# High and low weight tiles ahead of the token tiles, and two of the second feed-forward's five pairs in a pool of its own

## The chip, the cores and the metric

The kernel runs on one core of one Trainium2 chip. The metric is the device time of one execution in microseconds (us); lower is better. Engines are named as in the profile: PE is TensorE, DVE is VectorE, ACT is ScalarE, POOL is GpSimd, SP is SyncE, which issues the loads of the weights.

## The reference, cut to what matters

One block on 256 tokens of width 2048, in fp32: a feed-forward (width 5632), a mixer (S5 recurrence and pooling), cross attention to 256 memory tokens, a second feed-forward, and a last norm. The change touches the place of the weight tiles in all of it, and the work of the second feed-forward and its surroundings:

```python
def swiglu(x, w_gate, w_up, w_down):
    return (jax.nn.silu(x @ w_gate) * (x @ w_up)) @ w_down
...
    return o @ w_o          # end of the memory cross attention
```

The block ends as h = h + 0.5 * swiglu(rmsnorm(h), w2_gate, w2_up, w2_down), and then the last rmsnorm.

## The kernel before, in words

Every fp32 product is made of three products of rounded parts: a high part (fp32r) and the low rest. Weights come from HBM as 1 MB tiles `raw` (pool `wraw`, three buffers, 24 KB of each partition), by loads that SP issues (line 147). Each is split in two halves of 256 columns by `parts` (lines 136 to 143): ACT makes the high half `whi` by a copy (line 140), DVE the low half `wlo` by a subtraction (line 141). One `whi` with its `wlo` is called a pair here; each takes 8 KB of a partition. A pair feeds twelve matmuls in `tok_block` (lines 149 to 156: 2 blocks of columns x 2 halves of the tokens x 3 products, lines 154, 155, 156), with a token or activation tile `x` as the stationary operand and the weights as the moving one, 512 wide. In the middle of the block `load_w` and `block` (lines 103 to 120) use the same buffers the other way round, with the weights stationary.

Tile pools lie one behind the other in each partition, in the order in which they are opened: `const`, `wraw`, `xp` (16 token tiles of 2 KB), `actp` (12 activation tiles of 2 KB), `ev` (small buffers), and then `whl` with three pairs. Before the second feed-forward `whl` is closed (line 1008) and a pool `whl2` of five pairs is opened in its place (line 1009); a tile of a new pool waits until all users of the old one's room are done.

The order of instructions on each engine is set by a scheduler from dependencies and pools; it is not written out by hand. Semaphore waits follow from that order.

The end of the cross attention (lines 999 to 1003) is four groups of w_o; each ends with `add_to_h` (lines 256 to 262: DVE adds two accumulators to `h`) and `squares` (lines 231 to 236: ACT, names evq and ssq). `layer_in` (lines 244 to 254) transposes `h` on PE (line 251) into the next stage's token tiles.

The second feed-forward has eleven chunks f of 512 columns. Chunks 0 and 1 go through `plain` (line 1023). The other nine go through `seven` (line 1088), in which sums of quarters let seven products do the work of eight: `product` (lines 1055 to 1062) takes six matmuls from a pair, with quarters of token tiles or the sums `SH` and `SL` as the stationary operand; `eight` (line 1106) is the plain way for the rest. `SH`, `SL` and the temporaries lie in a pool `sw` behind the others (line 1067). Down passes for finished chunks are taken in between (accumulators `dacc`). The last down pass, of chunk 10 alone, runs after `sw` is closed (line 1177): four groups n of one raw tile, eight pairs in all, each group followed by `add_to_h` (line 262), `squares` and, one group later, `columns` (lines 1167 to 1175: eight transposes, four copies `o`).

Of the kernel before, what the change touches and what calls it, by code (L numbers as in the profile page):

```python
# [9 lines left out]
F32R = mybir.dt.float32r  # L10
# [4 lines left out]
P = 128  # L15
# [32 lines left out]
def rev2(ap3):  # L48

    (ps, pn), (s, n), inner = ap3.ap[0], ap3.ap[1], ap3.ap[2]  # L50
    return bass.AP(tensor=ap3.tensor, offset=ap3.offset + s * (n - 1), ap=[[ps, pn], [-s, n], list(inner)])
# [3 lines left out]
def block_kernel(ctx: ExitStack, tc: tile.TileContext, xT, memT, wgu1, wd1, w_in, w_glu, w_pool, w_out,  # L55
# [3 lines left out]

    const = ctx.enter_context(tc.tile_pool(name="const", bufs=1))  # L60
    wraw = ctx.enter_context(tc.tile_pool(name="wraw", bufs=3))
    xp = ctx.enter_context(tc.tile_pool(name="xp", bufs=16))
    ap_ = ctx.enter_context(tc.tile_pool(name="actp", bufs=12))
    ev = ctx.enter_context(tc.tile_pool(name="ev", bufs=2))
    parted = ExitStack()
    whl = parted.enter_context(tc.tile_pool(name="whl", bufs=3))
    banks = ExitStack()
    psA = banks.enter_context(tc.tile_pool(name="psA", bufs=6, space=bass.MemoryType.PSUM))
    psB = banks.enter_context(tc.tile_pool(name="psB", bufs=2, space=bass.MemoryType.PSUM))
# [18 lines left out]
    ssq = const.tile([P, 2, 2 * ND], F32, name="ssq")  # L88
    A8R = const.tile([P, 2, 32], F32, name="A8R")
    A8I = const.tile([P, 2, 32], F32, name="A8I")  # L90

    def vcol(c):
        return vec[:, c:c + 1]


    def wsplit(r, n, out=None):

        hi, lo = out or [whl.tile([P, 1024], F32R, name=m) for m in ("whi", "wlo")]
        S.activation(out=hi[:, :n], in_=r, func=AF.Copy)  # L99
        V.tensor_tensor(out=lo[:, :n], in0=r, in1=hi[:, :n].bitcast(F32), op=ALU.subtract)  # L100
        return hi, lo
# [28 lines left out]
    def wtile(load):  # L130

        raw = wraw.tile([P, 4, 512], F32, name="raw")
        load(raw)
        return parts(raw)

    def parts(raw):
        blocks = []
        for c in (0, 256):
            hi, lo = (whl.tile([P, 4, 256], F32R, name=m) for m in ("whi", "wlo"))
            S.activation(out=hi, in_=raw[:, :, c:c + 256], func=AF.Copy)  # L140
            V.tensor_tensor(out=lo, in0=raw[:, :, c:c + 256], in1=hi.bitcast(F32), op=ALU.subtract)  # L141
            blocks += [(hi[:, :, j:j + P], lo[:, :, j:j + P]) for j in (0, P)]
        return blocks
# [69 lines left out]
    def spread(col, out):  # L213

        dg = ev.tile([P, L], F32, name="dg", bufs=1)
        for j in range(2):
            V.tensor_scalar(out=dg[:, j * P:(j + 1) * P], in0=ident, scalar1=col[:, j:j + 1], scalar2=None, op0=ALU.mult)
        pb = psB.tile([P, 2 * L], F32, name="psb")
        T.matmul(pb[:, :L], ones, dg, start=True, stop=True)
        S.activation(out=out, in_=pb[:, :L], func=AF.Copy)  # L220
# [17 lines left out]
    def norm_of_h():  # L238
        v = ev.tile([P, 2], F32, name="rv")
        V.reduce_sum(out=v, in_=ssq, axis=mybir.AxisListType.X)  # L240
        V.tensor_scalar(out=v, in0=v, scalar1=1.0 / D, scalar2=EPS, op0=ALU.mult, op1=ALU.add)
        newton(rcol, v)
# [97 lines left out]
    def s5_tables(pp):  # L340
# [10 lines left out]
        def tt(o, a, b, op):  # L351
            tc.keep_in_program_order(V.tensor_tensor(out=o, in0=a, in1=b, op=op))
# [71 lines left out]
        def factors(ar, ai, k):  # L424
            V.tensor_copy(out=ar[:, 0], in_=PW[:, k, 0])
            V.tensor_copy(out=ar[:, 1], in_=PW[:, k, 0])
            ts(ai[:, 0], PW[:, k, 1], -1.0, ALU.mult)
            V.tensor_copy(out=ai[:, 1], in_=PW[:, k, 1])

        factors(ARm, AIm, 1)  # L430
        for k in range(1, 8):
# [4 lines left out]
            tt(PW[:, k + 1], PW[:, k + 1], T1, ALU.add)  # L436
        factors(A8R, A8I, 8)
        PR = pp.tile([P, 8, 2, 32], F32, name="PR")
# [191 lines left out]
    with ExitStack() as c2:  # L630
# [108 lines left out]
        def recur(c):  # L739
            T1 = mp.tile([P, 2, 32], F32, name="rec1", bufs=2)  # L740
            T2 = mp.tile([P, 2, 32], F32, name="rec2", bufs=2)
            G.tensor_tensor(out=T1, in0=XS[:, :, c - 1], in1=A8R, op=ALU.mult)
            G.tensor_tensor(out=T2, in0=rev2(XS[:, :, c - 1]), in1=A8I, op=ALU.mult)
            G.tensor_tensor(out=T1, in0=T1, in1=T2, op=ALU.add)
# [21 lines left out]
        def k_group():  # L766
            accs = [psA.tile([P, 2 * L], F32, name="acc") for _ in range(4)]

            def halves():
                for kq in range(4):  # L770
                    raw = wraw.tile([P, 2048], F32, name="raw")
                    nc.sync.dma_start(out=raw, in_=w_k[kq])
                    for c in (0, 1024):
                        yield wsplit(raw[:, c:c + 1024], 1024)

            parts = halves()
            ahead = [next(parts)]
            for k in range(KT):
                if k % 2 == 0:
                    ahead.append(next(parts, None))  # L780
                    hi, lo = ahead.pop(0)
                for n in range(4):
                    c = (k % 2 * 4 + n) * P
                    block(accs[n], (hi[:, c:c + P], lo[:, c:c + P]), ms[k], k == 0, k == KT - 1)
                if k == 7:
                    pool_out(0)
                recurs(1)
            for n in range(4):
                total(accs[n], out=kT[:, n])
# [115 lines left out]
    with ExitStack() as c3:  # L905
# [64 lines left out]
        for cg in range(4):  # L970
            accs = [psA.tile([P, 2 * L], F32, name="acc") for _ in range(2)]
            for kq in range(4):
# [4 lines left out]
                for half in range(2):  # L977
                    hi, lo = wsplit(raw[:, half * 1024:(half + 1) * 1024], 1024)
# [26 lines left out]


    banks.close()
    parted.close()
    whl = ctx.enter_context(tc.tile_pool(name="whl2", bufs=5))
    psA = ctx.enter_context(tc.tile_pool(name="psC", bufs=4, space=bass.MemoryType.PSUM))  # L1010
    psB = ctx.enter_context(tc.tile_pool(name="psD", bufs=2, space=bass.MemoryType.PSUM))
    fe = ctx.enter_context(tc.tile_pool(name="fe2", bufs=2))
# [23 lines left out]
    def down(a, b, acts, accs_of=tok_accs, done=None):  # L1036

        for n in range(ND):
            accs = accs_of()
            for i, f in enumerate(range(a, b)):  # L1040
                blocks = wtile(cols4(wd2[f, 4 * n:4 * n + 4], 0))
                flush()
                for j, w in enumerate(blocks):
                    tok_block(accs, w, acts[4 * i + j], i + j == 0, f == b - 1 and j == 3)
                if f == b - 1:
                    add_to_h(accs, n, qcol)
                    if done is not None:
                        done(n)
                yield
# [15 lines left out]
        return lambda j: [xf[k + j][:, i * L + lt * P:i * L + (lt + 1) * P] for i in range(2)]  # L1065

    with tc.tile_pool(name="sw", bufs=1) as sw:
        SH = sw.tile([P, 4, 4, P], F32R, name="SH")
        SL = sw.tile([P, 4, 4, P], F32R, name="SL")

        def token_sums():
# [9 lines left out]
            for o in (0, 2):  # L1081
                S.activation(out=SH[:, o:o + 2], in_=s[:, o:o + 2], func=AF.Copy)
                V.tensor_tensor(out=SL[:, o:o + 2], in0=s[:, o:o + 2], in1=SH[:, o:o + 2].bitcast(F32), op=ALU.subtract)

        def tsum(o):
            return lambda j: (SH[:, o, j], SL[:, o, j])

# [62 lines left out]
        for a, b in PASSES2:  # L1150
# [10 lines left out]
            if b < FC:  # L1161
                steps = down(a, b, acts, lambda: [psA.tile([P, 512], F32, name="dacc", bufs=2) for _ in range(2)])

    with tc.tile_pool(name="last", bufs=1) as last:
        o = last.tile([P, KT, L], F32, name="o")

        def columns(n):

            for k in (4 * n, 4 * n + 2):
                pt = psB.tile([P, 2, L], F32, name="psb")  # L1170
                for j in range(2):
                    for lt in range(2):
                        T.transpose(pt[:, j, lt * P:(lt + 1) * P], h[:, lt, (k + j) * P:(k + j + 1) * P], ident)
                for j in range(2):
                    S.activation(out=o[:, k + j], in_=pt[:, j], func=AF.Copy, scale=vcol(G_FINAL + k + j))

        for n, _ in enumerate(down(*PASSES2[-1], acts, done=squares)):
            if n > 0:
                columns(n - 1)
        columns(ND - 1)  # L1180
        norm_of_h()
        spread(rcol, Ra)
        for k in range(0, KT, 4):
            V.tensor_tensor(out=o[:, k:k + 4], in0=o[:, k:k + 4], in1=Ra.unsqueeze(1).to_broadcast([P, 4, L]), op=ALU.mult)
            (nc.sync if k % 8 == 0 else nc.scalar).dma_start(out=outT[:, k:k + 4], in_=o[:, k:k + 4])
# [81 lines left out]
```

## Time and profile before

| | us |
|---|---|
| median of three runs | 2163.28 |
| lowest, highest | 2163.13, 2164.45 |
| the profiled execution | 2161.42 |
| its span | 2159.6 |
| PE busy in the span | 2123.0 (98%) |
| DVE busy | 1503.1 (70%) |
| ACT busy | 1075.8 (50%) |
| granted TensorE clock, mean | 0.994 |

The profile shows one execution. Times in its rows count from the start of the span; the execution's own time is 1.8 us longer than the span. Matmuls overlap: a row of one matmul lasts about 0.4 us, but the next one starts some 0.23 us after it, so pace is read from one start to the next. A row of several instructions gives the start of the first and the time to the end of the last. The number in brackets behind a row is the time for which the engine stood idle just before, and what ended that.

### The profile page before, as it was taken

What the parts mean: (1) busy time and instruction counts of PE and PEld (TensorE: products, weight loads), DVE (VectorE), ACT (ScalarE), POOL (GpSimd) and SP (SyncE); (2) the same over time, 40 slices, a digit from 0 to 9 for tenths busy, and PEclk for the clock granted to TensorE, in tenths of its full rate; (3) what the DMA queues carried; (4) which work ended last, traced back from release to release, by engine and by line L of the source; (5) the groups of instructions that cost most, each with busy time, mean ns of one, the idle gap of its engine ahead of it and who ended that gap; (6) DMA issues with size and microseconds to landing.
All of it is one profiled execution on the core that took longest, in us unless ns stands there. A gap on an engine that the chain in (4) does not pass through costs nothing.

```text
span 2159.6 us, 26792 instructions
## 1 busy us (share of the span) xinstructions
PE 2123.0 (98%) x10248; PEld 1736.6 (80%) x10248; DVE 1503.1 (70%) x2021; ACT 1075.8 (50%) x1510; POOL 141.3 (7%) x255
## 2 busy tenths in 40 slices
PE   9999999999999999979999999999999999999997
PEld 7888888788888888868888888878888888888885
DVE  6566766666555667836767755566888888888874
ACT  6443444344444555625655644544555555555543
POOL 0000011111100001750000000000000000000000
PEclk9999999999999999989999999999999999999998
DMA  7665777677766657768545556657565566565542
GB/s 244 206 182 189 203 207 217 220 215 214 217 215 186 219 189 242 247 205 261 187 164 176 196 175 208 198 155 222 175 205 182 186 210 209 179 199 187 181 154 94
DMA packets 202320, 427.58 MB, mean 198 GB/s; under 512 B 17872, under 2 KB 31376, under 8 KB 193104
## 3 DMA queue, kind: packets, MB, share of 16 engines
q1 hardware_dynamic: 181280, 392.35, 57.5%
q0 software_dynamic: 6416, 18.85, 3.0%
q10 hardware_dynamic: 14496, 14.68, 2.2%
q8 instruction: 80, 1.31, 0.2%
q14 instruction: 48, 0.39, 0.0%
HBM read 408.05 MB, written 16.78 MB: 197 GB/s over the span
## 4 chain that ended last, share of the span: by engine, by line
PE 93%; POOL 3%; DMA 1%; DVE 1%; ACT 1%; issue 1%; SPq 0%; DVEq 0%; ACTq 0%
PE acc L156 19%; PE acc L155 19%; PE acc L154 19%; PE acc L119 7%; PE acc L120 4%; PE dacc L154 3%; PE dacc L155 3%; PE dacc L156 3%; PE psb L1062 2%; PE psb L1060 2%; PE psb L1061 2%; PE acc L985 1%; PE acc L986 1%; PE acc L984 1%; PE acc L1062 1%; PE acc L1060 1%
## 5 line engine op out<-in xcount | busy, mean ns | idle before, releaser
L141 DVE TENSOR_TENSOR wlo<-raw,whi 128x1024 fp32r<-128x1024 f32 x522 | 636.4, 1224 | 374.1 <-ACT whi L140 371.0
L140 ACT ACTIVATE whi<-raw 128x1024 fp32r<-128x1024 f32 x522 | 552.9, 1060 | 662.9 <-PE acc L156 483.5
L155 PE MATMUL acc<-wlo,x 128*128 128x512 f32 x1760 | 697.7, 397 | 0.3 <-DVE wlo L141 0.3
L156 PE MATMUL acc<-whi,x 128*128 128x512 f32 x1760 | 695.8, 396 | 0.0
L154 PE MATMUL acc<-whi,x 128*128 128x512 f32 x1760 | 643.9, 397 | 0.0
L156 PEld LDWEIGHTS acc<-whi,x 128*128 128x128 f32 x1760 | 331.9, 189 | 77.5 <-issue 1.2
L155 PEld LDWEIGHTS acc<-wlo,x 128*128 128x128 f32 x1760 | 331.9, 189 | 77.5 <-DVE wlo L141 0.9
L154 PEld LDWEIGHTS acc<-whi,x 128*128 128x128 f32 x1760 | 331.2, 189 | 76.3 <-issue 0.6
L119 PE MATMUL acc<-x,whi 128*128 128x512 f32 x848 | 299.8, 397 | 3.1 <-ACT whi L99 3.1
L100 DVE TENSOR_TENSOR wlo<-raw,whi 128x1024 fp32r<-128x1024 f32 (+1 forms) x144 | 172.0, 1199 | 124.5 <-ACT whi L99 108.9
L120 PE MATMUL acc<-x,wlo 128*128 128x256 f32 x848 | 236.7, 285 | 1.0 <-DVE wlo L100 0.9
L99 ACT ACTIVATE whi<-raw 128x1024 fp32r<-128x1024 f32 (+1 forms) x144 | 146.9, 1023 | 153.9 <-PE acc L119 93.6
L119 PEld LDWEIGHTS acc<-x,whi 128*128 128x128 f32 x848 | 158.8, 188 | 40.3 <-ACT whi L99 5.4
L120 PEld LDWEIGHTS acc<-x,wlo 128*128 128x128 f32 x848 | 158.8, 189 | 5.5 <-DVE wlo L100 2.6
L156 PE MATMUL dacc<-whi,x 128*128 128x512 f32 x320 | 127.0, 397 | 0.0
L154 PE MATMUL dacc<-whi,x 128*128 128x512 f32 x320 | 125.9, 398 | 0.9 <-DVE h L262 0.9
L155 PE MATMUL dacc<-wlo,x 128*128 128x512 f32 x320 | 126.4, 395 | 0.0
L140 ACT ACTIVATE whi<-t 128x1024 fp32r<-128x1024 f32 x54 | 57.4, 1063 | 53.2 <-PE acc L156 32.6
L141 DVE TENSOR_TENSOR wlo<-t,whi 128x1024 fp32r<-128x1024 f32 x54 | 64.9, 1225 | 23.3 <-ACT whi L140 22.4
L141 DVE TENSOR_TENSOR wlo<-r,whi 128x1024 fp32r<-128x1024 f32 x54 | 65.9, 1220 | 15.7 <-ACT whi L140 15.6
L140 ACT ACTIVATE whi<-r 128x1024 fp32r<-128x1024 f32 x54 | 56.2, 1058 | 37.0 <-PE acc L156 15.6
L154 PEld LDWEIGHTS dacc<-whi,x 128*128 128x128 f32 x320 | 60.4, 189 | 14.5 <-issue 1.3
(276 smaller groups left out, 2139.4 us busy)
## 6 DMA issues: line engine op xcount, KB each, us to landing
raw<-in_wgu SPq DMA_DIRECT2D x148, 1024.0 KB, 6.1
raw<-in_wd SPq DMA_DIRECT2D x88, 1024.0 KB, 5.3
r<-in_wgu SPq DMA_DIRECT2D x27, 1024.0 KB, 6.1
raw<-in_w_in SPq DMA_DIRECT2D x16, 1024.0 KB, 5.0
raw<-in_w_k SPq DMA_DIRECT2D x16, 1024.0 KB, 5.4
raw<-in_w_out SPq DMA_DIRECT2D x32, 512.0 KB, 5.1
raw<-in_w_q SPq DMA_DIRECT2D x16, 1024.0 KB, 4.9
raw<-in_w_v SPq DMA_DIRECT2D x16, 1024.0 KB, 4.9
```

What stands on the lines that cost most here:

```text
L99: S.activation(out=hi[:, :n], in_=r, func=AF.Copy)
L100: V.tensor_tensor(out=lo[:, :n], in0=r, in1=hi[:, :n].bitcast(F32), op=ALU.subtract)
L119: T.matmul(acc, w[0], x, start=first, stop=False)
L120: T.matmul(acc[:, :L], w[1], x[:, :L], start=False, stop=last)
L140: S.activation(out=hi, in_=raw[:, :, c:c + 256], func=AF.Copy)
L141: V.tensor_tensor(out=lo, in0=raw[:, :, c:c + 256], in1=hi.bitcast(F32), op=ALU.subtract)
L154: T.matmul(acc, xh, w[0], start=first, stop=False)
L155: T.matmul(acc, xh, w[1], start=False, stop=False)
L156: T.matmul(acc, xl, w[0], start=False, stop=last)
L1060: T.matmul(acc, xh, wh, start=first and j == 0, stop=False)
L1061: T.matmul(acc, xh, wl, start=False, stop=False)
L1062: T.matmul(acc, xl, wh, start=False, stop=last and j == 3)
```

## The change

The pool `whl` is opened ahead of `xp`, and is never closed; three pairs stay in it through the whole kernel. `parts` takes its pair from the pools of a list `pairs` in turn. While `sw` is open the list is whl, sw, whl, sw, whl, so that five pairs are in rotation, two of them in `sw`. In the last down pass, behind `sw`, the list is `whl` alone: three pairs. `xp`, `actp` and `ev` lie 24 KB further on than before. Each engine has the same number of instructions of each kind, and SP's and POOL's orders are the same. Line numbers after the change are one or two higher.

```diff
     wraw = ctx.enter_context(tc.tile_pool(name="wraw", bufs=3))
+    whl = ctx.enter_context(tc.tile_pool(name="whl", bufs=3))
     xp = ctx.enter_context(tc.tile_pool(name="xp", bufs=16))
     ap_ = ctx.enter_context(tc.tile_pool(name="actp", bufs=12))
     ev = ctx.enter_context(tc.tile_pool(name="ev", bufs=2))
-    parted = ExitStack()
-    whl = parted.enter_context(tc.tile_pool(name="whl", bufs=3))
...
+    pairs = [whl]
...
         for c in (0, 256):
-            hi, lo = (whl.tile([P, 4, 256], F32R, name=m) for m in ("whi", "wlo"))
+            pairs.append(pairs.pop(0))
+            hi, lo = (pairs[-1].tile([P, 4, 256], F32R, name=m, bufs=3 if pairs[-1] is whl else 2) for m in ("whi", "wlo"))
...
     banks.close()
-    parted.close()
-    whl = ctx.enter_context(tc.tile_pool(name="whl2", bufs=5))
...
     with tc.tile_pool(name="sw", bufs=1) as sw:
+        pairs[:] = [whl, sw, whl, sw, whl]
...
+    pairs[:] = [whl]
     with tc.tile_pool(name="last", bufs=1) as last:
```

ACT where the last w_o tile ends and the second feed-forward begins. Before (the third `whi` is the last tile of w_o, first half; the fifth is the first of the second feed-forward):

```order
L189 ACTIVATE x<-psb,vec 128x256 [waits PE_49]
L140 ACTIVATE whi<-raw 128x1024 [waits PE_49]
L189 ACTIVATE x<-psb,vec 128x256 [waits DVE_49]
L140 ACTIVATE whi<-raw 128x1024 [waits DMAHW6_49,PE_49,Activation_49]
L140 ACTIVATE whi<-raw 128x1024 [waits PE_49,Activation_49]
L140 ACTIVATE whi<-raw 128x1024 [waits DMAHW7_49,DVE_49,PE_49]
L140 ACTIVATE whi<-raw 128x1024
L140 ACTIVATE whi<-raw 128x1024 [waits DMAHW0_49]
L236 ACTIVATE evq,ssq<-h 128x256 [waits DVE_49]
```

And after:

```order
L191 ACTIVATE x<-psb,vec 128x256 [waits PE_49]
L142 ACTIVATE whi<-raw 128x1024 [waits PE_49]
L142 ACTIVATE whi<-raw 128x1024 [waits DMAHW7_49]
L191 ACTIVATE x<-psb,vec 128x256 [waits DVE_49]
L142 ACTIVATE whi<-raw 128x1024 [waits DMAHW6_49,PE_49,Activation_49]
L142 ACTIVATE whi<-raw 128x1024 [waits PE_49,Activation_49]
L142 ACTIVATE whi<-raw 128x1024 [waits DMAHW0_49]
L142 ACTIVATE whi<-raw 128x1024 [waits DVE_49,PE_49] x2
L142 ACTIVATE whi<-raw 128x1024 [waits DMAHW1_49,DVE_49,PE_49]
L238 ACTIVATE evq,ssq<-h 128x256 [waits DVE_49]
```

The `whi` that waits for DMAHW7 is the second feed-forward's first tile; one half of it has moved ahead of the two `whi` of w_o's last tile, and one of the next tile right behind them, both into pairs of `sw`.

PE at the same place. Before:

```order
L156 MATMUL acc<-whi,x 128x512
L251 MATMUL psb<-ident,h 128x128 [waits DVE_49]
L251 MATMUL psb<-ident,h 128x128
L251 MATMUL psb<-ident,h 128x128 [waits DVE_49]
L251 MATMUL psb<-ident,h 128x128 x5
L154 MATMUL acc<-whi,x 128x512 [waits Activation_49]
L154 MATMUL acc<-whi,x 128x512
L155 MATMUL acc<-wlo,x 128x512 [waits DVE_49]
```

And after:

```order
L158 MATMUL acc<-whi,x 128x512
L253 MATMUL psb<-ident,h 128x128 [waits DVE_49]
L253 MATMUL psb<-ident,h 128x128
L156 MATMUL acc<-whi,x 128x512 [waits DVE_49,Activation_49]
L157 MATMUL acc<-wlo,x 128x512
L158 MATMUL acc<-whi,x 128x512
...
L253 MATMUL psb<-ident,h 128x128 x6
L156 MATMUL acc<-whi,x 128x512 [waits Activation_49]
```

Six of the eight transposes now stand behind the first 72 matmuls of the second feed-forward.

ACT in one of the nine chunks of `seven` (numbers behind a name tell tiles apart; `s5` is a copy of a product). Before:

```order
L140 ACTIVATE whi_16487<-raw_16485 128x1024 [waits DMAHW6_49,PE_49]
L1117 ACTIVATE s5_16309<-psb_16403 128x512 [waits PE_49]
L140 ACTIVATE whi_16491<-raw_16485 128x1024
L140 ACTIVATE whi_16522<-r12_16399 128x1024 [waits PE_49,Activation_49]
L140 ACTIVATE whi_16526<-r12_16399 128x1024 [waits DVE_49,PE_49]
```

And after:

```order
L142 ACTIVATE whi_16487<-raw_16481 128x1024 [waits DMAHW6_49,PE_49]
L1118 ACTIVATE s5_16305<-psb_16399 128x512 [waits PE_49]
L142 ACTIVATE whi_16483<-raw_16481 128x1024
L142 ACTIVATE whi_16518<-r12_16395 128x1024 [waits PE_49,Activation_49]
L142 ACTIVATE whi_16522<-r12_16395 128x1024 [waits DVE_49,PE_49]
```

The lower number of two is the tile that the program names first. Of this raw tile the half that comes first in the program (16483) is now made second; DVE's two `wlo` are exchanged in the same way. It is so in all nine chunks. In each, one L1060 of the product that follows also stands eleven matmuls earlier on PE.

## Rows read from the trace of the kernel before

**Rows 1.** Page, part 1: busy us of each engine (share of span) xinstructions
```profile
PE 2123.0 (98%) x10248; PEld 1736.6 (80%) x10248; DVE 1503.1 (70%) x2021; ACT 1075.8 (50%) x1510; POOL 141.3 (7%) x255
```

**Rows 2.** Windows: length, busy PE PEld DVE ACT POOL (xcount), clock, DMA share, GB/s
```profile
1416.00:1440.00 24.00, 23.38 (x104) 18.18 (x103) 17.79 (x32) 15.06 (x24) 0.00 (x0) 1.00 0.68 209
1500.00:1600.00 100.00, 100.00 (x441) 81.18 (x440) 82.99 (x86) 52.65 (x59) 0.00 (x0) 1.00 0.58 181
```

**Rows 3.** Waits of 1385 to 1440: total us, times, longest
```profile
ACT whi L140 <- DVE h L260: 7.2, 1, 7.2
```

**Rows 4.** Timeline of ACT, start of the second feed-forward: start, us, what
```profile
1408.91 1.06 ACT L140 ACTIVATE whi<-raw 128x1024 fp32r<-128x1024 f32 x1 [1.74 <-PE acc L156]
1417.22 2.96 ACT L140 ACTIVATE whi<-raw 128x1024 fp32r<-128x1024 f32 x3 [7.25 <-DVE h L260]
```

**Rows 5.** Timeline of DVE, same place
```profile
1410.00 1.22 DVE L141 TENSOR_TENSOR wlo<-raw,whi 128x1024 fp32r<-128x1024 f32 x1 [1.58 <-ACT whi L140]
1416.52 1.39 DVE L260 TENSOR_TENSOR h<-acc,h 128x512 f32<-128x512 f32 x2 [5.30 <-PE acc L156]
1418.31 3.50 DVE L141 TENSOR_TENSOR wlo<-raw,whi 128x1024 fp32r<-128x1024 f32 x3 [0.40 <-ACT whi L140]
```

**Rows 6.** Timeline of PE, same place
```profile
1416.79 0.40 PE L156 MATMUL acc<-whi,x 128*128 128x512 f32 x1
1417.27 0.44 PE L251 MATMUL psb<-ident,h 128*128 128x128 f32 x2
1417.97 0.88 PE L251 MATMUL psb<-ident,h 128*128 128x128 f32 x6 [0.26 <-DVE h L260]
1418.60 0.72 PE L154 MATMUL acc<-whi,x 128*128 128x512 f32 x2
1419.59 0.50 PE L155 MATMUL acc<-wlo,x 128*128 128x512 f32 x1 [0.27 <-DVE wlo L141]
1419.93 0.39 PE L156 MATMUL acc<-whi,x 128*128 128x512 f32 x1
```

**Rows 7.** Timeline of SP's queue: loads issued, 1395 to 1440
```profile
1399.17 37.02 SPq L147 DMA_DIRECT2D raw<-in_wgu  x8
```

**Rows 8.** Page, part 6: issues of a load, KB each, us to landing
```profile
raw<-in_wgu SPq DMA_DIRECT2D x148, 1024.0 KB, 6.1
```

**Rows 9.** Timeline of ACT in one chunk of the seven products
```profile
1655.37 1.06 ACT L140 ACTIVATE whi<-raw 128x1024 fp32r<-128x1024 f32 x1 [2.59 <-PE psb L1062]
1657.23 1.05 ACT L140 ACTIVATE whi<-raw 128x1024 fp32r<-128x1024 f32 x1
1658.18 2.00 ACT L140 ACTIVATE whi<-r 128x1024 fp32r<-128x1024 f32 x2
```

**Rows 10.** Timeline of DVE in the same chunk
```profile
1658.32 1.23 DVE L141 TENSOR_TENSOR wlo<-raw,whi 128x1024 fp32r<-128x1024 f32 x1 [0.62 <-ACT whi L140]
```

**Rows 11.** Timeline of PE in the same chunk
```profile
1659.79 0.64 PE L154 MATMUL acc<-whi,x 128*128 128x512 f32 x2
1660.27 0.39 PE L155 MATMUL acc<-wlo,x 128*128 128x512 f32 x1
1663.04 0.40 PE L1060 MATMUL psb<-whi,SH 128*128 128x512 f32 x1
```

**Rows 12.** Timeline of ACT in the last down pass: its last whi
```profile
2126.76 1.06 ACT L140 ACTIVATE whi<-raw 128x1024 fp32r<-128x1024 f32 x1
```

**Rows 13.** Timeline of PE there: the first matmuls of two pairs
```profile
2123.77 0.39 PE L154 MATMUL acc<-whi,x 128*128 128x512 f32 x1
2126.56 0.39 PE L154 MATMUL acc<-whi,x 128*128 128x512 f32 x1
```

**Rows 14.** Timeline of PE: first and last of twelve matmuls with SH, SL
```profile
1625.50 0.39 PE L1060 MATMUL acc<-whi,SH 128*128 128x512 f32 x1
1627.99 0.40 PE L1062 MATMUL acc<-whi,SL 128*128 128x512 f32 x1
```

**Rows 15.** Page, part 5: one of the three lines of tok_block, all acc
```profile
L155 PE MATMUL acc<-wlo,x 128*128 128x512 f32 x1760 | 697.7, 397 | 0.3 <-DVE wlo L141 0.3
```

## The prediction

> **What bounds the kernel now.** I read the page first: PE is busy for 2123.0 us of the 2159.6 us span, 98% of it, and DVE for 70% [rows 1]. Time can only go where PE stands still, or where its matmuls come at another pace. So I asked for the busy time by stage. In the second feed-forward PE has no gap at all: 100.00 us busy of 100, while DVE is busy for 82.99 of them; the stretch in which that stage begins has 23.38 of 24.00 [rows 2]. The 0.62 us missing there are the one place before the last stage that the change touches and where PE stands. The waits of that stretch name the cause on ACT: 7.2 us for the additions to h [rows 3]. I then read the timelines of ACT, DVE and PE at three places where the orders differ: this start, the chunks of the seven products, and the last down pass.
>
> **Start of the second feed-forward.** Before, the first pair of the new pool cannot be made until the old pool is given up, which is when the last additions to h (line 260) are done. ACT ends the last pair of w_o at 1409.97, then stands 7.25 us until 1417.22 [rows 4]. DVE stands 5.30 us ahead of the two additions (1416.52, 1.39 us) and makes its first wlo from 1418.31 [rows 5]. PE begins its last w_o matmul at 1416.79, does eight transposes, two L154 at 1418.60, and only at 1419.59 the first L155; the third kind begins at 1419.93 [rows 6]. PE's pace, from the tail, is 12 matmuls in 2126.56 - 2123.77 = 2.79 us, 0.2325 each [rows 13]. The two L154 from 1418.60 would end at about 1419.07 by that pace; L155 began 0.52 later, and the six transposes waited 0.26 for the second addition [rows 6].
>
> After, four FFN2 pairs (two of them in the new pool of the stage, two in the old buffers as w_o leaves them) are made before the additions. Is the data there? The first wgu load is issued at 1399.17 [rows 7] and such a load takes 6.1 us to land [rows 8]: 1405.3. One whi of FFN2 now goes in ahead of w_o's last raw tile on ACT and costs it at most 1.06 us; ACT's last w_o whi stood 1.74 us for PE before [rows 4], so it is covered. DVE has to make four wlo of 1.23 us, 4.9 us, in its 5.30 us of idleness [rows 5]; the third and fourth need buffers that PE frees one pair (2.79 us) and two pairs before its end, so the fourth can run until about 1416.7 and push the additions by some 0.2 us, to 1416.7 to 1418.1. The accumulators need both additions, so I let the first FFN2 matmul begin at 1418.1, after two of the eight transposes. At 1419.93 PE has then done (1419.93 - 1418.1) / 0.2325 = 7.9 matmuls where before it had done three: 4.9 x 0.2325 = 1.1 us ahead. Six transposes come later instead: 1418.60 - 1417.97 = 0.63 us [rows 6]. **Sum of this place: -0.5 us.** Bounds: -1.2 (all that lies between the last matmul's end, about 1417.02, and 1419.59, less 1.3 us of transposes and two L154), and +1.2 if DVE's fourth wlo (1.23) stands fully ahead of the additions.
>
> **The nine chunks of seven products.** The number of pairs stays five and no instruction is added. In each chunk one raw tile has its halves split in the other order: the second half goes first, and the half that PE wants first is ready when the second was. Before, ACT makes the two at 1655.37 and 1657.23 [rows 9], DVE the later one at 1658.32 for 1.23 us, to 1659.55 [rows 10]. PE wants the whi at 1659.79 and the wlo at 1660.27 [rows 11]. **Cover 0.7 us, so cost nothing.** One product matmul (L1060, 1663.04) also moves ahead by 11 matmuls, 2.6 us, to about 1660.4 [rows 11]; its whi is the first of two that ACT does from 1658.18, so about 1659.2 [rows 9]. Cover about 1 us.
>
> **The last down pass with three pairs.** With three in rotation a pair is made again while PE reads the other two: 2 x 2.79 = 5.6 us [rows 13]. Making one takes ACT 1.06 and DVE 1.23, 2.5 us with the hand-overs. Before, with five, the last whi began at 2126.76 [rows 12], the moment after PE took up the pair at 2126.56 [rows 13]. Now it waits for two later pairs and stands behind squares and copies, and its DVE half behind two additions of about 1.39 [rows 5]. 2.5 + 1.4 leaves 1.7 us of cover. **Cost 0**; upper end: four squares and four copies of 128x256 on ACT, each a quarter of a whi's elements, at half a whi's time (an estimate, 8 x 0.53 = 4.2 us) all in one turn-round, which makes that pair 4.2 - 1.7 = 2.5 us late.
>
> **Addresses in the front half.** Ahead of the second feed-forward every instruction and wait is the same; the pair buffers change places with the token tiles, the activation tiles and the small buffers. No row shows this move. Token tiles as stationary operands run at 0.2325 [rows 13]. The sums SH and SL, which lie behind the pair buffers, run at (1627.99 - 1625.50) / 11 = 0.2264 [rows 14], in the same form of matmul. So position may bear on the pace. I take 0 for the sum, because 0.2325 holds for tiles over a wide stretch of addresses in front; ends: -32 us if 5280 matmuls [rows 15] all gained 6.1 ns, and nothing known on the other side.
>
> **Sum:** -0.5 + 0 + 0 + 0 = -0.5 us. The profiled execution took 2161.42 us, so it would be 2160.9; the median of the runs is 1.9 above it, 2163.28, and I predict against the median: 2162.8. A measurement of this kernel tells some 0.2%, 4.3 us, from no change.
>
> [...]
>
> **Rivals.**
> 1. *Place sets the pace.* Pairs now lie in front of token tiles in the whole front half and for three of five pairs in FFN2; if a stationary tile behind its moving one is the faster case, as SH is, up to 32 us go. For it: rows 14. Against it: nothing shows that it is position and not something else about these tiles, and two of five pairs stay behind. I price it at half, 16 us: 2147. Sign: PE busy 100.00 of 100, but more matmuls in each such window. Chance 0.28.
> 2. *Slower: the swapped halves come too late.* One mechanism, nine times: if the first-used half's wlo ends more than 0.7 us after 1659.55 in its chunk, PE stands at L155. One more DVE instruction of 1.23 ahead of it [rows 10] makes 0.53 us a chunk, 4.8 us in nine, 2167.6; two make 1.76 a chunk, 15.8 us, 2178.6. The point is 0.7 us. For it: DVE is the next busiest engine in this stage, 83% [rows 2]. Against it: its order here is otherwise the same. Chance 0.08. A pace lowered by the new addresses adds 0.04.
> 3. *The start gains nothing:* PE still waits for the additions and then for something else. 2163.3, in the same class as the forecast.
>
> **How the numbers follow.** Forecast with rival 3: 0.60, its own range 2160 to 2167 (bounds +1.2 and +2.5 of the start and the tail, a few us for the spread of runs). Rival 1: 0.28, from 2131 to 2160, mostly above 2147. Rival 2 and the slower pace: 0.12, of which a third stays under 2168. The range 2147 to 2168 leaves out about half of rival 1 and most of rival 2, some 0.2. Faster by over 0.2% (under 2159.0): 0.29, a part of rival 1 being too small to count and some luck added. Slower (over 2167.6): 0.11. Same: 0.60.
>
> **What would show it.** Right: ACT's gap of 7.25 us is gone, a whi of FFN2 stands ahead of the last w_o pair, L155 follows its L154 with no wait at about 1418.5; busy share of PE still 100 of 100 in the chunks; no wait of PE for a whi or wlo after 2110. Wrong: twelve matmuls of token tiles that take clearly less (or more) than 2.79 us anywhere in the first 1400 us; a wait of PE for wlo in each chunk; a wait for whi in the last four pairs.

## The result, and the profile after

The changed kernel takes 2138.31 us (median of four runs, 2135.02 to 2138.39) against 2163.86 us of the kernel before on the same chip (four runs, 2163.13 to 2165.43): 0.9875 of it, 95% interval 0.9864 to 0.9887, about 25 us less. The forecast was 2162.8 with a range down to 2147. The first rival (place sets the pace) had the direction; its point was 2147, and its range, 2131 to 2160, holds the result.

The first lines of the page after, which answer to [rows 1]: the span is 23.0 us shorter, and PE's busy time fell by 27.2 us with the same number of instructions.

```profile
span 2136.6 us, 26778 instructions
...
PE 2095.8 (98%) x10248; PEld 1731.6 (81%) x10248; DVE 1502.9 (70%) x2021; ACT 1077.2 (50%) x1510; POOL 141.5 (7%) x255
```

The time went where no wait was. Windows of the kernel before: the first feed-forward from 60 to 620, the middle of the block from 620 to 1300, and most of the second feed-forward from 1500 to 2060. Behind the two lengths stand busy time and count of PE.

```profile
60.00:620.00 560.00, 560.00 (x2579) 450.85 (x2578) 365.67 (x514) 236.82 (x275) 48.49 (x87) 1.00 0.69 207
620.00:1300.00 680.00, 663.80 (x3703) 555.57 (x3702) 443.62 (x731) 358.50 (x607) 90.23 (x161) 0.99 0.63 204
1500.00:2060.00 560.00, 560.00 (x2453) 455.10 (x2452) 479.27 (x496) 300.19 (x328) 0.00 (x0) 1.00 0.61 192
```

The same windows of the kernel after:

```profile
60.00:620.00 560.00, 560.00 (x2633) 459.95 (x2633) 372.06 (x524) 243.16 (x281) 50.78 (x90) 1.00 0.71 213
620.00:1300.00 680.00, 661.00 (x3721) 555.83 (x3720) 442.79 (x727) 359.69 (x609) 88.13 (x157) 0.99 0.63 204
1500.00:2060.00 560.00, 560.00 (x2468) 457.31 (x2467) 483.54 (x502) 304.53 (x332) 0.00 (x0) 1.00 0.61 190
```

In the first and the last window PE is busy for all 560.00 us in both kernels, at a granted clock of 1.00. After, it does 54 more instructions in the first, 2.1%, and 15 more in the last, 0.6%. The first lies in the part in which each instruction and each wait is the same as before. One token tile's stretch of the first feed-forward, on PE, before (twelve matmuls from the first row to the second):

```profile
100.21 0.40 PE L156 MATMUL acc<-whi,x 128*128 128x512 f32 x1
...
103.01 0.40 PE L156 MATMUL acc<-whi,x 128*128 128x512 f32 x1
```

And after, twelve matmuls too:

```profile
99.97 0.39 PE L158 MATMUL acc<-whi,x 128*128 128x512 f32 x1
...
102.69 0.39 PE L156 MATMUL acc<-whi,x 128*128 128x512 f32 x1
```

That is 2.80 / 12 = 0.233 before and 2.72 / 12 = 0.227 after. So by the last w_o matmul the kernel is 16.1 us ahead (1416.79 in [rows 6], 1400.67 below), and the second feed-forward and the end bring the other 6.9 of the 23.0.

The start of the second feed-forward after, on PE, answering to [rows 6]:

```profile
1400.67 0.39 PE L158 MATMUL acc<-whi,x 128*128 128x512 f32 x1
1401.35 0.44 PE L253 MATMUL psb<-ident,h 128*128 128x128 f32 x2 [0.29 <-DVE h L262]
1402.04 0.47 PE L156 MATMUL acc<-whi,x 128*128 128x512 f32 x1 [0.25 <-DVE h L262]
1402.35 0.39 PE L157 MATMUL acc<-wlo,x 128*128 128x512 f32 x1
```

ACT there, answering to [rows 4], and DVE, answering to [rows 5]:

```profile
1398.38 1.06 ACT L142 ACTIVATE whi<-raw 128x1024 fp32r<-128x1024 f32 x1 [0.49 <-PE acc L158]
1401.43 1.06 ACT L142 ACTIVATE whi<-raw 128x1024 fp32r<-128x1024 f32 x1 [1.99 <-DMA raw<-in_wgu]
```

```profile
1396.97 3.73 DVE L143 TENSOR_TENSOR wlo<-raw,whi 128x1024 fp32r<-128x1024 f32 x3 [1.66 <-ACT whi L142]
1400.62 1.28 DVE L262 TENSOR_TENSOR h<-acc,h 128x512 f32<-128x512 f32 x2
```

ACT's gap of 7.25 us is gone, and L157 follows its L156 without a wait. DVE comes to the additions straight from a wlo, and PE waits 0.29 and 0.25 us for them. All of PE's waits from 1420 to the end, after:

```profile
PE psb L221 <- DVE dg L219: 2.9, 1, 2.9
PE psb L1175 <- ACT o L1177: 1.5, 2, 1.0
PE dacc L156 <- DVE h L264: 1.0, 1, 1.0
```

None is for a whi or a wlo: neither the swapped halves nor the three pairs of the last pass are ever late.

### The profile page after: what moved, and what is told of

Read it like the earlier page. It is cut to its first block, busy times and chain, and to the rows that moved or that the text cites. A ratio compares the mean times of both kernels' runs of the same rounds, so it can differ in the third digit from the quotient of the medians.

```text
span 2136.6 us, 26778 instructions
## 1 busy us (share of the span) xinstructions
PE 2095.8 (98%) x10248; PEld 1731.6 (81%) x10248; DVE 1502.9 (70%) x2021; ACT 1077.2 (50%) x1510; POOL 141.5 (7%) x255
## 4 chain that ended last, share of the span: by engine, by line
PE 92%; POOL 3%; DMA 2%; DVE 1%; ACT 1%; issue 1%; SPq 0%; DVEq 0%; ACTq 0%; POOLq 0%
PE acc L158 19%; PE acc L156 19%; PE acc L157 19%; PE acc L120 6%; PE dacc L156 3%; PE dacc L157 3%; PE dacc L158 3%; PE acc L121 3%; PE psb L1060 2%; PE psb L1062 2%; PE psb L1061 2%; PE acc L987 1%; PE acc L988 1%; PE acc L986 1%; PE acc L1062 1%; PE acc L1060 1%
## 5 line engine op out<-in xcount | busy, mean ns | idle before, releaser
L157 PE MATMUL acc<-wlo,x 128*128 128x512 f32 x1760 | 689.7, 392 | 0.0
L158 PE MATMUL acc<-whi,x 128*128 128x512 f32 x1760 | 688.2, 392 | 0.0
L156 PE MATMUL acc<-whi,x 128*128 128x512 f32 x1760 | 637.7, 393 | 0.3 <-DVE h L262 0.3
L157 PEld LDWEIGHTS acc<-wlo,x 128*128 128x128 f32 x1760 | 331.2, 188 | 70.1 <-issue 0.4
L156 PEld LDWEIGHTS acc<-whi,x 128*128 128x128 f32 x1760 | 330.5, 188 | 70.2 <-issue 1.1
L156 PE MATMUL dacc<-whi,x 128*128 128x512 f32 x320 | 124.9, 395 | 1.0 <-DVE h L264 1.0
L157 PE MATMUL dacc<-wlo,x 128*128 128x512 f32 x320 | 125.3, 391 | 0.0
L156 PEld LDWEIGHTS dacc<-whi,x 128*128 128x128 f32 x320 | 60.1, 188 | 14.0 <-issue 1.4
```

Of the source, the lines that this page charges most:

```text
L156: T.matmul(acc, xh, w[0], start=first, stop=False)
L157: T.matmul(acc, xh, w[1], start=False, stop=False)
L158: T.matmul(acc, xl, w[0], start=False, stop=last)
```

## The experiments

**Theories at this point.** Theory 1: a matmul is faster when its stationary operand lies behind its moving one within some 84 KB. It was made from the pace of single tiles in both traces, which isn't shown here. Theory 2: the gain is in the new order and the pool that is never given up.

**A grid of places, by itself.** The kernel's body is replaced by twelve tiles and this loop over all pairs of them:

```diff
+    for s in range(12):
+        for m in range(12):
+            acc = [psA.tile([P, 512], F32, name=n) for n in ("even", "odd")]
+            for i in range(24):
+                x = tiles[s][:, 3, (i % 4) * P:(i % 4 + 1) * P]
+                T.matmul(acc[i % 2], x, tiles[m][:, 4], start=i < 2, stop=i > 21)
```

> Leaves out the whole computation; only PE's pace is read. Twelve tiles of 16 KB, A to L, lie one behind the other in a partition, and each of the 144 pairs (stationary tile, moving tile) runs 24 matmuls of 128x512 with nothing else on ACT, DVE or the DMA queues. Theory 1 (place: a matmul is faster when its stationary operand lies behind its moving one by less than some 84 KB, five tiles): about 0.228 us a matmul for stationary tiles one to five places behind the moving one, about 0.2325 for the rest, the stationary tile ahead of the moving one or six and more behind. Theory 2 (place has no part in it; SH, SL and the changed kernel are faster by what ACT, DVE and the loads do at the time): one pace for all 144 pairs, within 1 ns. Theory 3 (only the moving operand's own address counts): the pace changes with the moving tile alone.

PE's timeline there; the first name is the moving tile, the second the stationary one. First and last of 24 matmuls, with F moving and A stationary, and the other way round:

```profile
39.16 0.39 PE L75 MATMUL even<-tF,tA 128*128 128x512 f32 x1
...
44.38 0.39 PE L75 MATMUL odd<-tF,tA 128*128 128x512 f32 x1
...
338.36 0.39 PE L75 MATMUL even<-tA,tF 128*128 128x512 f32 x1
...
343.58 0.39 PE L75 MATMUL odd<-tA,tF 128*128 128x512 f32 x1
```

Both take 5.22 / 23 = 0.227. So do all pairs (0.2265 to 0.2270) but A with itself, which comes first and has its engine's start in it. ACT was still writing tiles up to 49.4 us, during the first of these two; the second, at 338 us, had PE to itself. Order and distance alone do nothing. This left open whether they matter only beside other work.

**The three pairs in other places.** Order and waits are the changed kernel's on every engine; only addresses differ. First behind the small buffers, as before:

```diff
     wraw = ctx.enter_context(tc.tile_pool(name="wraw", bufs=3))
-    whl = ctx.enter_context(tc.tile_pool(name="whl", bufs=3))
     xp = ctx.enter_context(tc.tile_pool(name="xp", bufs=16))
     ap_ = ctx.enter_context(tc.tile_pool(name="actp", bufs=12))
     ev = ctx.enter_context(tc.tile_pool(name="ev", bufs=2))
+    whl = ctx.enter_context(tc.tile_pool(name="whl", bufs=3))
```

> The changed kernel with the three pairs opened behind the small buffers again, the two pairs in the stage's pool kept; every engine's order is that of the changed kernel, word for word. Theory 1 (place of the pairs): no token tile lies behind its pair, so all is lost but the start's 0.4 us: 2163 to 2165, twelve matmuls of token tiles in 2.79 us. Theory 2 (the gain is in the new order, the pool that is never given up, and the pairs in turn): 2138.

Measured: 2164.26 us (ten runs), 0.9996 of before (0.9986 to 1.0005). Its first window:

```profile
60.00:620.00 560.00, 560.00 (x2578) 450.55 (x2577) 365.46 (x514) 236.86 (x274) 48.49 (x86) 1.00 0.70 207
```

2578 instructions, as before. Theory 2 falls: the whole of the change but the place of `whl` is here, and nothing is gained that this comparison can tell.

Then between the token tiles and the activation tiles:

```diff
     wraw = ctx.enter_context(tc.tile_pool(name="wraw", bufs=3))
-    whl = ctx.enter_context(tc.tile_pool(name="whl", bufs=3))
     xp = ctx.enter_context(tc.tile_pool(name="xp", bufs=16))
+    whl = ctx.enter_context(tc.tile_pool(name="whl", bufs=3))
```

> The changed kernel with the three pairs between the token tiles (in front) and the activation tiles (behind); order as in the changed kernel. Theory 1: of 6948 matmuls with a token or activation tile as stationary operand 2344 lie behind their pair by less than 84 KB (5850 in the changed kernel): 2164 - 2344 x 0.0049 = 2152.5, between 2150 and 2155, with down passes at 0.228 and gate and up products of the first feed-forward at 0.2325. Theory 2: 2138. Theory 3 (the moving operand's own address alone): gate and up products at the same pace as down products.

Measured: 2138.11 us, 0.9874 of before (0.9856 to 0.9891), where theory 1 said 2150 to 2155.

```profile
60.00:620.00 560.00, 560.00 (x2634) 459.87 (x2633) 372.74 (x525) 242.36 (x280) 50.64 (x90) 1.00 0.70 212
```

The first feed-forward has all of its pace, with its token tiles ahead of the pairs. Theory 1 falls. And ahead of the raw tiles:

```diff
     const = ctx.enter_context(tc.tile_pool(name="const", bufs=1))
+    whl = ctx.enter_context(tc.tile_pool(name="whl", bufs=3))
     wraw = ctx.enter_context(tc.tile_pool(name="wraw", bufs=3))
-    whl = ctx.enter_context(tc.tile_pool(name="whl", bufs=3))
```

> The changed kernel with the three pairs ahead of the raw weight tiles, 24 KB further to the front; order as in the changed kernel. Theory 1 with its upper limit of some 84 KB: 1172 matmuls of the rear activation tiles fall out of reach: 2138.3 + 1172 x 0.0049 = 2144, between 2141 and 2146, the slower ones in the down passes. If the only thing that counts is that the stationary tile lies behind: 2138. Theory 2: 2138.

Measured: 2136.67 us, 0.9868 (0.9854 to 0.9883). No loss at a distance either; the upper limit of 84 KB was wrong too.

**The third theory.** What the slow place alone has is what lies ahead of it: the small buffers of `ev`. The addresses of tiles in the compiled programs, in bytes of a partition, and their remainder by 256:

```
                     first token tile   first whi (three pairs)   SH
before               61792   96         122336  224               171488  224
after                86368   96          61792   96               155104  224
behind              as before            as before
between              61792   96          94560   96
ahead of raw tiles   86368   96          37216   96
```

`ev` holds two buffers of 1024 bytes, four columns of 32 and one of 1024: 3200 bytes, 12 x 256 + 128. All other pools between are multiples of 2 KB. So whatever stands behind `ev` is 128 bytes out of line with the token tiles in front of it (in line means: the same remainder by 256). In each fast kernel the three pairs are in line with the token tiles, in each slow one out of line; and before, SH was in line with the pairs and fast [rows 14]. In the grid all tiles were in line. Theory A: what counts is whether the addresses of moving and stationary operand agree in their last bits. Theory B, the rival that was left: place or distance, felt only beside other work.

**Offsets, by themselves.** The grid's loop with the moving operand pushed by `mo`, the stationary one by `so` elements of 4 bytes:

```diff
-                x = tiles[s][:, 3, (i % 4) * P:(i % 4 + 1) * P]
-                T.matmul(acc[i % 2], x, tiles[m][:, 4], start=i < 2, stop=i > 21)
+                x0, w0 = 1024 + so + i % 4 * P, 2048 + mo
+                T.matmul(acc[i % 2], rows[0][:, x0:x0 + P], rows[1][:, w0:w0 + 512], start=i < 2, stop=i > n - 3)
```

> Leaves out the whole computation; only PE's pace is read, with nothing else at work. 48 groups of 24 matmuls of 128x512: the moving operand pushed by 0, 128, ... 1408 bytes against a stationary one that stays; the stationary one pushed in the same steps; both pushed together; the moving one pushed in steps of 32 bytes. Theory A (relative alignment: the two operands' addresses in the partition must agree in their last bits): 0.227 a matmul where the push is a multiple of some round number (256 or 512 bytes), about 0.2325 at 128, 0.227 throughout where both are pushed together. Theory B (distance or order in the partition, only felt when ACT, DVE and the loads are at work): 0.227 everywhere.

First and last of 24 matmuls each, on PE's timeline: moving operand pushed by 128 bytes (tG,tB) and by 256 (tH,tC); stationary operand by 128 (tI,tB); both by 128 (tD,tB); moving operand by 32 (tE,tB) and by 64 (tF,tC):

```profile
35.60 0.40 PE L76 MATMUL even<-tG,tB 128*128 128x512 f32 x1
...
40.96 0.39 PE L76 MATMUL odd<-tG,tB 128*128 128x512 f32 x1
41.19 0.39 PE L76 MATMUL even<-tH,tC 128*128 128x512 f32 x1
...
46.42 0.39 PE L76 MATMUL odd<-tH,tC 128*128 128x512 f32 x1
...
101.88 0.40 PE L76 MATMUL even<-tI,tB 128*128 128x512 f32 x1
...
107.24 0.40 PE L76 MATMUL odd<-tI,tB 128*128 128x512 f32 x1
...
168.16 0.39 PE L76 MATMUL even<-tD,tB 128*128 128x512 f32 x1
...
173.38 0.40 PE L76 MATMUL odd<-tD,tB 128*128 128x512 f32 x1
...
233.56 0.40 PE L76 MATMUL even<-tE,tB 128*128 128x512 f32 x1
...
238.93 0.40 PE L76 MATMUL odd<-tE,tB 128*128 128x512 f32 x1
239.16 0.40 PE L76 MATMUL even<-tF,tC 128*128 128x512 f32 x1
...
244.43 0.39 PE L76 MATMUL odd<-tF,tC 128*128 128x512 f32 x1
```

Over 23 steps that is 0.2330 for a moving operand pushed by 128 bytes, 0.2274 for 256, 0.2330 for the stationary one by 128, 0.2270 for both together, 0.2335 for 32 and 0.2291 for 64. The steps of 128 bytes go on like this up to 1408 for either operand: 0.2326 to 0.2335 for odd ones, 0.2270 to 0.2274 for even ones (the first group, at no push, has its engine's start in it). During the groups up to 46.4 us ACT was still writing tiles (its last row ends at 49.54). Behind that PE is alone; the window of the stationary operand pushed by 128 bytes, with ACT and POOL at 0.00 and no DMA to speak of:

```profile
101.80:107.30 5.50, 5.50 (x26) 4.44 (x25) 0.00 (x0) 0.00 (x0) 1.00 0.01 3
```

So with nothing else at work PE's pace depends on the difference of its two addresses by 256 bytes: 0.227 in line, up to 0.234 out of line. It is no contention with other engines. Nor is it the moving operand's own address (theory 3 of the grid): a push of the stationary one alone costs as much, and a push of both costs nothing.

**In the kernels.** First 384 bytes left free behind `ev` in the kernel before; the same line in the changed kernel is the next run.

```diff
-    ev = ctx.enter_context(tc.tile_pool(name="ev", bufs=2))
+    ev = ctx.enter_context(tc.tile_pool(name="ev", bufs=2)); ctx.enter_context(tc.tile_pool(name="gap", bufs=1)).tile([P, 96], F32, name="gap")
```

> The kernel before with 384 bytes left free behind the small buffers and nothing else changed: the pairs stay behind the token tiles, in one line with them (all addresses leave 352 when divided by 512; before, the pairs left 480). Theory A: 6948 matmuls with token or activation tiles gain 4.9 ns less what 848 pairs of matmuls with stationary weights may lose: 2163.9 - 33 = 2131, between 2129 and 2138. Theory B: 2164.

> The changed kernel with 384 bytes left free behind the small buffers: the stage's own two pairs, SH, SL and the memory's token tiles come into line with the rest; the three pairs in front are in line already. Theory A: 1002 matmuls with 4.9 ns, 96 with 5 and 270 with SH or SL with 2.8 to gain: 2138.3 - 6 = 2132. Theory B: 2138.

And 128 bytes between `whl` and the token tiles of the changed kernel:

```diff
-    whl = ctx.enter_context(tc.tile_pool(name="whl", bufs=3))
+    whl = ctx.enter_context(tc.tile_pool(name="whl", bufs=3)); ctx.enter_context(tc.tile_pool(name="gap", bufs=1)).tile([P, 32], F32, name="gap")
```

> The changed kernel with 128 bytes left free between the three pairs and the token tiles: place and order are the changed kernel's, but token and activation tiles are out of line with the three pairs. Theory A: the 5850 matmuls go back to 0.2325, those with the stage's own pairs come into line: 2138.3 + 28.7 - 5 = 2162, between 2158 and 2166. Theory B: 2138.

| kernel | us | of before (95%) |
|---|---|---|
| before, 384 bytes free | 2128.05 | 0.9833 (0.9819 to 0.9848) |
| changed, 384 bytes free | 2128.59 | 0.9836 (0.9821 to 0.9850) |
| changed, 128 bytes free | 2164.14 | 0.9996 (0.9987 to 1.0006) |

Theory A holds three times out of three. In the third its forecast was 2162, with 5 us to be gained by the pairs in `sw`. That part was wrong: the gap pushes them along with the token tiles, so these stay 128 bytes apart, and the second window shows no gain (2451 matmuls below, 2453 before). The windows of the kernel before with its 384 bytes:

```profile
60.00:620.00 560.00, 560.00 (x2633) 459.78 (x2632) 372.74 (x525) 242.27 (x280) 50.79 (x90) 1.00 0.70 212
...
1500.00:2060.00 560.00, 560.00 (x2503) 463.59 (x2502) 488.55 (x507) 307.26 (x332) 0.00 (x0) 1.00 0.62 195
```

The changed kernel with 384:

```profile
60.00:620.00 560.00, 560.00 (x2632) 459.80 (x2632) 372.54 (x525) 242.47 (x281) 50.79 (x90) 1.00 0.71 212
...
1500.00:2060.00 560.00, 560.00 (x2503) 463.73 (x2502) 489.05 (x508) 307.77 (x335) 0.00 (x0) 1.00 0.62 194
```

And the changed kernel with 128:

```profile
60.00:620.00 560.00, 560.00 (x2580) 451.14 (x2579) 365.18 (x512) 237.51 (x274) 48.64 (x86) 1.00 0.69 208
...
1500.00:2060.00 560.00, 560.00 (x2451) 454.41 (x2450) 478.55 (x495) 299.58 (x328) 0.00 (x0) 1.00 0.60 190
```

The unchanged kernel with a gap has the changed kernel's pace in the first window and does better in the second: 2503 against 2468, since the changed kernel's two pairs in `sw` lie behind `ev` and stay out of line with the token tiles, and SH and SL came out of line with the three pairs in front. The changed kernel with a gap has 2503 too. Both run some 9 us faster than the changed kernel as it stands (0.9833 and 0.9836 of before against 0.9875) and cannot be told from one another. They came out some 3 us below what was expected (2131 and 2132). For the kernel before, the size fits: the mean step between matmuls with token or activation tiles is 0.2326 before and 0.2272 with the gap, 5.4 ns; 6852 such matmuls came into line, which makes 37 us, and measured were 2165.0 - 2128.05 = 37.

**What the two more pairs carry.** The changed kernel with 384 bytes and three pairs alone in the second feed-forward:

```diff
-        pairs[:] = [whl, sw, whl, sw, whl]
+        pairs[:] = [whl]
```

> The changed kernel with the 384 bytes free, and in the second feed-forward the three pairs in front alone, without the stage's own two. If the two more pairs carry nothing (as the last down pass, which has three, shows no wait): 2127 to 2131, as with five. Rival: in the seven products PE uses up a pair in six matmuls, 1.36 us, and making one takes ACT and DVE some 2.5 us, so that three pairs leave hardly any cover and PE waits for whi or wlo in each chunk: 2135 to 2160, with all of the difference between 1470 and 2060.

Measured: 2152.09 us, some 23 us more than with five pairs; its first window is the same as theirs. The rival holds, but for two details: PE waits for a wlo in eight of the nine chunks, and one wait for a whi (1.6 us, ending at 1448) comes ahead of them. PE's waits for pairs there, from 1395 on:

```profile
PE acc L157 <- DVE wlo L143: 16.0, 8, 3.1
...
PE acc L156 <- ACT whi L142: 1.6, 1, 1.6
```

The window 1500 to 2060 has PE busy for 543.96 us and a count of 2406:

```profile
1500.00:2060.00 560.00, 543.96 (x2406) 446.39 (x2405) 476.45 (x491) 297.91 (x323) 0.00 (x0) 0.99 0.62 187
```

The waits add to 17.6 us. Part of the other 6 or so is the clock. Behind two of the eight waits, of 3.09 and 2.18 us, the granted clock stands at 0.50 for 3.41 us each, where it is 1.00 in this stage of the other kernels. The first of the two, and PE's rows in it:

```profile
1680.30:1683.70 3.40, 3.17 (x8) 2.50 (x9) 3.40 (x4) 0.00 (x0) 0.00 (x0) 0.50 0.18 31
```

```profile
1680.53 0.79 PE L157 MATMUL acc<-wlo,x 128*128 128x512 f32 x1 [3.09 <-DVE wlo L143]
1681.12 0.63 PE L158 MATMUL acc<-whi,x 128*128 128x512 f32 x1
1681.54 0.63 PE L157 MATMUL acc<-wlo,x 128*128 128x512 f32 x1
```

The matmuls step at 0.42 to 0.43 there, against 0.227 at 1.00. Half of 2 x 3.41 us is 3.4 us, an estimate of what that costs. Some 2 us stay open.

The kernel before with its gap ran once more beside it:

> The kernel before with its 384 bytes free once more, on the same chip as the one ahead. If order and pairs are worth what the start shows and no more (0.3 to 0.5 us): 2127 to 2131.

Measured: 2129.56 us (median of three), 0.9844 of before (0.9825 to 0.9864). A fourth execution took 4577.87 us; what held it up is not known, and it is left out of both.

## Why the prediction was wrong, point by point

- **Addresses in the front half: the step that failed.** "I take 0 for the sum, because 0.2325 holds for tiles over a wide stretch of addresses in front." All those tiles were out of line with the pairs by the same 128 bytes, so they could only agree with one another. The row that differed, SH at 0.2264 [rows 14], was the pace in line, and 0.2325 [rows 13] the pace out of line. The evidence was in hand, and the sum took 0 from it; it went into rival 1 at half of its price. By count: in the changed kernel 5850 matmuls with token or activation tiles read a pair of `whl`; by some 4.9 ns, the difference of the mean step between such matmuls over the whole traces (0.2326 before, about 0.2277 after in line), that is 28.7 us. Against it, 1002 that read `sw` pairs gain nothing, and 96 with memory tiles and 270 of 432 with SH or SL have come out of line: at the same 4.9 ns they lose 1.8 us. PE also stood 2.8 us longer in the middle of the block (663.80 and 661.00 busy of 680) and 1.3 us longer in the first 60 us (54.89 and 53.59 busy). The idle time there varies between kernels of one order: with the pairs between token and activation tiles the middle has 664.11. 28.7 - 1.8 - 2.8 - 1.3 = 22.8, and the start of the second feed-forward gives another 0.3 (below): 23.1, against 23.0 by which the span fell. That is closer than the mean step is good for: 0.1 ns of it is 0.6 us.
- **Rival 1** named the right thing, place, with the wrong rule (behind or ahead), and so the wrong size. The end of -32 was no bound on place: it counted the 5280 matmuls of `tok_block` into `acc` alone, and the kernel before with its gap gained 37 us on 6852. Half between the ends was chosen without a row, so its 2147 is not a measure of the effect.
- **The start:** -0.5 forecast. Taken in the two kernels with 384 bytes, where the pace is the same in both: from the last w_o matmul to the fourth matmul of the stage 3.13 us before (1397.69 to 1400.82) and 2.15 after (1400.63 to 1402.78), less 0.67 us for the six transposes that come later. That makes -0.3 us. The mechanism was right; as forecast, DVE came to the additions some 0.2 us late from a wlo, and PE waited for them (0.68 us from the last matmul's start to the transposes, 0.48 before).
- **The nine chunks** and **the last down pass:** 0 forecast for each, and no wait of PE for a pair anywhere in them. Right.
- **Rival 2** (the swapped halves too late) did not come. What it said of DVE as the next bound was shown by the run with three pairs, which lost 16.0 us to PE's waits for a wlo, and more to the clock behind them.

## What to carry to other kernels

Where PE is busy all the time, look at the step from one matmul to the next in several places, and when two stretches of the same form differ (0.2264 and 0.2325 here), find what differs before the rest of the kernel is tuned: 2.6% of every matmul is more than most waits that are left. For matmuls of this form, give the tiles that are read as moving and as stationary operands addresses that agree by 256 bytes (the same remainder when divided by 256): in the offsets run the step was 0.2270 so, and 0.2330 at 128 bytes. Small buffers belong behind them, or their room is rounded up. A change that only moves pools can be tried against a gap of some bytes; if the gap does the same, the order of the pools was not the cause.

## What was not expected of the hardware

In the offsets run, with PE alone at work, 24 matmuls of 128x512 in fp32r took 0.2270 us each (up to 0.2277 right behind a slower group) when moving and stationary operand had the same address by 256 bytes, 0.2291 at 64 and 320 bytes, and 0.2326 to 0.2339 at the other offsets tried, in steps of 32. Pushed together by any of its steps they kept 0.2270; in the grid, at distances from 0 to 176 KB, either way round, the pace was 0.2265 to 0.2270. What in the engine makes it so stays open: no run was made for it. The trace of the offsets has a hint, in nanoseconds. Take the last matmul of a group whose own operands were in line. It stepped to the next group in 226 or 227 where the next group's stationary operand was in line with the moving one of this matmul too (seven groups), and in 232 or 233 where it was out of line (eighteen groups). So what counts may be the moving operand against the stationary operand of the next matmul. Matmuls with stationary weights, 512 and 256 wide in turn, were not measured by themselves.
